# One mixer's slot count, and two weight matrices used unsplit in fp32 products

## The chip, the cores and the metric

The kernel runs on one core of a Trainium2 chip. The metric is device time in microseconds (us) of one execution. The three executions shown of the kernel before took 1184.0, 1187.42 and 1192.24 us; their median is 1187.42 us.

## The reference

Two layers run over 256 tokens of width 1024, all in float32. Each layer is a SwiGLU feed-forward block, a token mixer and a second feed-forward block. Each block has an RMS norm before and after it, and shift, scale and gate vectors computed from a conditioning vector `c` (`silu(c) @ mod_w`). The mixer, in short:

```
proj = h @ w_in                       # cut into u, q, k, v, f, g_a, g_b
y_ssm = s5_ssm(u, ...)                # diagonal state-space scan, 32 groups of 64 states
z_val, z_gate = split(gelu(y_ssm) @ glu_w, 2)
y_a = z_val * sigmoid(z_gate)
attn = forgetting_attention(q, k, v, f + forget_b)      # 8 heads of 64
y_b = attn @ attn_w_out
out = (sigmoid(g_a) * y_a + sigmoid(g_b) * y_b) @ w_out
```

The two matrices that the change touches are `attn_w_out` (512 x 1024) and `glu_w` (512 x 2048), both in layer 0 only.

## The kernel before

**Pieces and their split.** All large weights are cut into pieces of 128 x 1024 float32 (512 KB) and stored in one tensor `ws` in the order in which they are wanted (`stream_order`, line 86). Class `Stream` (line 324) loads them one after the other through SyncE's queue (`pump`, tiles `raw`). A product in nearly full precision is made of three products in the type fp32r: ScalarE copies a piece into its rounded high part (`hi`, line 359), VectorE subtracts it to get the low part (`lo`, line 372), and `out_piece` (line 719) issues high x high, high x low and low x high for each half of 512 columns. The left operand is split in the same way. A piece of `mod_w` (`mod`) is not split: VectorE multiplies it by `silu(c)` and sums (tile `crow`).

**Slots.** Every 4 KB-per-partition tile lives in a pool of 42 slots. `used` counts one slot for a loaded piece and two for a split one. `room` is 42 less `KEPT` (what the current stage keeps for its own tiles) and, while the state-space tables are being built, less `TABLES[stage]`. `pump` loads while `used() < room()` and while fewer than 11 pieces wait loaded; `hi_at` makes no new split once `used() >= room()`, unless at most one split piece is unused.

**Order.** Each engine runs its instructions in the order in which they were written. That order is made while the program is built: class `Plan` keeps an estimated clock for each engine, and generators (`Task`) offer their next step with a rank; `pick` (line 223) takes the one that can start earliest, the lower rank in a tie.

**The mixer of layer 0** (`mix_body`, line 946). After the projections v, ga0, q, k and u, TensorE computes four rounds of attention scores (`sc`). While VectorE and ScalarE do their softmax, it fills in with the gate projections ga1, gb0 and gb1 (tiles `ga`, `gb`, four pieces each; `fill`) and with the state-space inputs `vr`, `vi`. The scan runs on VectorE (`zr`, `zi`); then come the products `ys`, in two halves by `states`, placed between the eight products of the attention output (`yb`, weights `ao`). The gelu of each half moves data in 16 small copies, alternately on VectorE and ScalarE (`gelu`, line 1283), then splits its result (`ygh`, `ygl`). `z` is the GLU product (weights `gl`); it needs gelu's first half for k = 0, 1 and its second from k = 2. Before the last product (`ym`, weights `mo`), `load_rows` (line 492) waits for the mixer's gate vector, and transposes it on TensorE (`gT`).

**The tables.** `s5_tables(0)` (line 1712) runs beside the first feed-forward block and the projections. Near its end `s5_place` writes table `d` to DRAM in 16 small DMAs; `load_tables` reads `bt` and `d` back into six slots; `s5_w` then builds the scan's phases `wc`, `ws` on VectorE, which go through DRAM to the scan.

Of the kernel before, what the change touches and what calls it, by code (L numbers as in the profile page):

```python
# [10 lines left out]
F32R = mybir.dt.float32r  # L11
I32 = mybir.dt.int32
AF = mybir.ActivationFunctionType
ALU = mybir.AluOpType
# [23 lines left out]
KEPT = {"ffn": 10, "mix0": 7, "mix1": 23, "mix2": 22, "mix3": 14, "mix4": 11}  # L38
TABLES = (11, 8)
TICKS = (1, 2)  # L40
# [5 lines left out]
NEAR = 1  # L46
LATER = 4
SCAN, GELU, MERGE, TR = 0.5, 0.95, 0.5, 1.5
# [37 lines left out]
def stream_order():  # L86
    order = []
    first = [("mod", 0, 0, r, k) for k in range(8) for r in (1, 0)]
    order += first[0:2] + [("fi", 0, 0, 0, 0)] + first[2:4]
    for n in range(1, 16):  # L90
        order += [("fi", 0, 0, n % 4, n // 4)] + first[3 + n:4 + n]
    mods = [
        vec(0, 0, 2) + vec(0, 1, 1) + vec(0, 1, 0),
        vec(0, 2, 1) + vec(0, 2, 0) + vec(0, 1, 2),
        vec(1, 0, 1) + vec(1, 0, 0) + vec(0, 2, 2) + vec(1, 1, 1),
        vec(1, 1, 0) + vec(1, 0, 2) + vec(1, 1, 2),
        [],
        vec(1, 2, 2),
    ]
    mods[2] += vec(1, 2, 1) + vec(1, 2, 0)  # L100
    for g in range(6):
        l, s = divmod(g, 3)
        w = sub_weights(l, s, g == 0)
        m = mods[g]
        lo, hi = SPREAD[0 if g == 0 else 1 + s % 2]
        hi += len(w)
        at = [lo + (hi - lo) * i // len(m) for i in range(len(m))]
        n = 0
        for i, key in enumerate(w):
            while n < len(m) and at[n] <= i:  # L110
                order.append(m[n])
                n += 1
            order.append(key)
        assert n == len(m)
    return order


# [206 lines left out]
class Stream:  # L324
    def __init__(self, kb, ws, order):
        self.kb, self.ws, self.order, self.plan = kb, ws, order, kb.plan
        self.dma = 0
        self.kept = KEPT["ffn"]
        self.hurry, self.over = None, []
        self.raw, self.mods, self.split = [], [], []  # L330
        self.live, self.fresh = {}, set()
        ahead = lambda: 0.4 if len(self.fresh) < NEAR else 1 if len(self.fresh) < AHEAD else 4
        Part(self.plan, self.hi_at, self.hi, ahead)
        Part(self.plan, self.lo_at, self.lo, ahead)
        Part(self.plan, self.mod_at, self.mod, self.mod_rank)

    def pump(self, most=None):
        kb, most = self.kb, most or RAW
        while self.dma < len(self.order) and len(self.raw) + len(self.mods) < most and self.used() < self.room():
# [4 lines left out]
            self.plan.floor = None  # L344
            (self.mods if key[0] == "mod" else self.raw).append((key, t))
            self.dma += 1

    def used(self):
        return len(self.raw) + len(self.mods) + 2 * (len(self.live) + len(self.split))

# [48 lines left out]
    def done(self, key):  # L399
        del self.live[key]  # L400
        self.pump()

# [11 lines left out]
class Kern:  # L414
# [304 lines left out]
    def out_piece(self, y, lh, ll, w, first, last):  # L719
        mm = self.nc.tensor.matmul  # L720
        wh, wl = w
        for n in range(2):
# [223 lines left out]
    def mix_body(self):  # L946
# [66 lines left out]
        self.probs_t(sc)  # L1013
        self.at = self.r4("ath", F32R), self.r4("atl", F32R)
        self.values(0, sc)
# [20 lines left out]
        def later_terms():  # L1036

            yg.extend([self.r4("yg"), self.r4("ygh", F32R), self.r4("ygl", F32R)])
            sr, si = s
# [65 lines left out]
        for m in range(2):  # L1105
            yb = self.psum("yb")
            for k in range(4):
                key = ("ao", l, k)
                w = self.st.need(key)
                a = k * 256 + m * P  # L1110
                self.out_piece(yb, self.at[0][:, a:a + P], self.at[1][:, a:a + P], w, k == 0, k == 3)
                if m == 1:
# [12 lines left out]
        for n, ms in ((0, (0, 1)), (1, (0,)), (1, (1,))):  # L1125
            z = {m: self.psum("z") for m in ms}
            for k in range(4):
# [4 lines left out]
                if n == 0 and k % 2 == 0:  # L1132
                    self.finish(late[k // 2])
                    if k == 2:
                        yg.pop(0)
                for m in ms:
                    a = k * 256 + m * P
                    self.out_piece(z[m], yg[-2][:, a:a + P], yg[-1][:, a:a + P], w, k == 0, k == 3)
                if ms[-1] == 1:
# [7 lines left out]
        if not turned:  # L1147
            self.finish(merges[0])
            self.transpose_split(0, [t[:, 0:512] for t in self.sga])
        self.merged = merges[1]  # L1150

    def load_tables(self):
# [130 lines left out]
    def gelu(self, h, ys, out):  # L1283

        nc = self.nc
        w = slice(512 * h, 512 * h + 512)
        y, hi, lo = (t[:, w] for t in out)
        yield "act", ys
# [4 lines left out]
        for b in range(4):  # L1293
            for t in range(4):
# [4 lines left out]
                else:  # L1299
                    yield "dve", g  # L1300
                    nc.vector.tensor_copy(o, i)
        yield "act", y
        nc.scalar.activation(hi, y, AF.Copy)
        yield "dve", hi
        nc.vector.tensor_tensor(lo, y, hi, op=ALU.subtract)

# [55 lines left out]
    def values(self, jt, sc):  # L1362
# [10 lines left out]
        def split():  # L1373
            src = ps.rearrange("p (m t) -> p m t", m=2)[:, :, 384:512]
            oh, ol = (t[:, 256 * jt:256 * jt + 256].rearrange("p (m t) -> p m t", m=2) for t in self.at)
            yield "act", ps
            nc.scalar.activation(oh, src, AF.Copy)
            yield "dve", self.plan.clk["act"] + self.plan.LATENCY
            nc.vector.tensor_tensor(ol, src, oh, op=ALU.subtract)
# [332 lines left out]
    def s5_tables(self, l):  # L1712
# [24 lines left out]
        kt = self.bd = self.cp = self.bc = None  # L1737
        if self.s == 1:
            self.load_tables()
        self.stage = 1  # L1740
# [220 lines left out]
```

## Time and profile before

| | us |
|---|---|
| median of the runs | 1187.42 |
| the profiled execution | 1182.35 |
| its span, first to last instruction | 1180.6 |
| TensorE busy in it | 1140.6 |
| VectorE busy in it | 912.7 |
| ScalarE busy in it | 608.6 |

"Busy" is time in which at least one instruction of the engine was running; in the profile PE is TensorE's products, PEld its weight loads, DVE is VectorE, ACT ScalarE and SP SyncE, whose queue issues the DMAs. Nearly every instruction has line 128, a helper through which all operations pass, so rows are told apart by the names of the tiles. The mean granted clock of TensorE over the span was 0.992 of full speed.

### The profile page before, as it was taken

The numbers are of one execution on the slowest core, as the hardware profiler recorded it, in microseconds if no ns is written. First come the engines' busy times: TensorE is split into PE (matmuls) and PEld (weight loads), VectorE is DVE, ScalarE is ACT, GpSimd is POOL, SyncE is SP. The second block draws the span as 40 slices with busy tenths as digits, with TensorE's granted clock in tenths as the row PEclk, the third lists the DMA queues.
The fourth block names the chain that finished last, engine by engine and source line by source line (L and its number), as shares of the span: only waits on it lengthen the run. The fifth ranks groups of instructions, "written<-read, shape, count | busy, mean of one in ns | idle before, by whom it ended". The sixth has DMA issues, their size and how long they took to land.

```text
span 1180.6 us, 19407 instructions
## 1 busy us (share of the span) xinstructions
PE 1140.6 (97%) x7488; PEld 1015.5 (86%) x7488; DVE 912.7 (77%) x1529; ACT 608.6 (52%) x943; POOL 36.2 (3%) x62
## 2 busy tenths in 40 slices
PE   8999999998998999999999999999999999999997
PEld 5999998796786779999979989987987887999995
DVE  6988987897998889999678878878448798855532
ACT  5653452685556564444364475356355756543421
POOL 1000000000000010000010000001000001000000
PEclk9999999998999999999999999999999999999999
DMA  9999887577887669999769398966645566765300
GB/s 361 408 367 407 301 286 267 187 257 236 339 306 249 224 235 390 360 376 381 246 214 355 127 330 284 373 248 237 227 127 179 180 212 216 284 224 204 126 19 36
DMA packets 99186, 306.50 MB, mean 260 GB/s; under 512 B 16373, under 2 KB 26133, under 8 KB 99094
## 3 DMA queue, kind: packets, MB, share of 16 engines
q1 hardware_dynamic: 99094, 305.27, 71.6%
q8 instruction: 58, 0.95, 0.3%
q14 instruction: 34, 0.28, 0.1%
HBM read 291.51 MB, written 13.71 MB: 259 GB/s over the span
## 4 chain that ended last, share of the span: by engine, by line
PE 86%; DVE 7%; ACT 3%; DMA 2%; issue 2%; POOL 1%; SPq 0%; DVEq 0%; POOLq 0%; ACTq 0%
PE f L128 35%; PE y L128 20%; PE n L128 5%; PE ym L128 3%; PE ga L128 3%; PE gb L128 3%; PE z L128 3%; PE k L128 2%; PE q L128 2%; PE v L128 2%; PE ys L128 2%; PE u L128 2%; ACT xh L128 1%; DVE raw L128 1%; PE yb L128 1%
## 5 line engine op out<-in xcount | busy, mean ns | idle before, releaser
L128 DVE TENSOR_TENSOR lo<-raw,hi 128x1024 fp32r<-128x1024 f32 x368 | 437.1, 1218 | 27.2 <-ACT hi L128 21.3
L128 ACT ACTIVATE hi<-raw 128x1024 fp32r<-128x1024 f32 x367 | 370.7, 1055 | 68.3 <-PE f L128 38.7
L128 PE MATMUL f<-xl,hi 128*128 128x256 f32 x1216 | 341.4, 281 | 2.7 <-DVE xl L128 2.7
L128 PE MATMUL f<-xh,hi 128*128 128x256 f32 x1216 | 342.0, 281 | 1.9 <-ACT xh L128 1.9
L128 PE MATMUL f<-xh,lo 128*128 128x256 f32 x1216 | 341.0, 280 | 0.0
L128 PEld LDWEIGHTS f<-xh,lo 128*128 128x128 f32 x1216 | 232.4, 191 | 0.0
L128 PEld LDWEIGHTS f<-xl,hi 128*128 128x128 f32 x1216 | 228.4, 188 | 4.6 <-DVE xl L128 3.6
L128 PEld LDWEIGHTS f<-xh,hi 128*128 128x128 f32 x1216 | 228.5, 188 | 3.8 <-ACT xh L128 2.5
L128 PE MATMUL y<-hi,ht 128*128 128x512 f32 x704 | 196.2, 391 | 0.8 <-DVE yg L128 0.8
L128 DVE SCALAR_TENSOR_TENSOR raw<-raw,crow 128x1024 f32<-128x1024 f32 x144 | 173.3, 1218 | 6.0 <-DMA raw<-ws 5.9
L128 PEld LDWEIGHTS y<-hi,ht 128*128 128x128 f32 x704 | 129.3, 188 | 26.2 <-DVE yg L128 1.1
L128 ACT ACTIVATE sg<-f 128x512 f32<-128x512 f32 x38 | 22.7, 597 | 222.7 <-PE f L128 215.4
L128 PE MATMUL y<-lo,ht 128*128 128x512 f32 x352 | 109.3, 390 | 0.8 <-ACT yg L128 0.8
L128 DVE TENSOR_TENSOR sg<-sg,f 128x512 f32<-128x512 f32 x38 | 26.1, 687 | 90.0 <-ACT sg L128 89.9
L128 PEld LDWEIGHTS y<-lo,ht 128*128 128x128 f32 x352 | 66.1, 188 | 15.1 <-ACT yg L128 1.2
L128 PE MATMUL n<-hi,xl 128*128 128x512 f32 x96 | 37.9, 395 | 1.7 <-DVE xl L128 1.7
L128 ACT ACTIVATE lg<-lg,st 128x128 f32<-128x128 f32 (+1 forms) x64 | 26.1, 444 | 25.3 <-DVE st L128 25.3
L128 PE MATMUL n<-hi,xh 128*128 128x512 f32 x96 | 38.4, 400 | 0.0
L128 PE MATMUL n<-lo,xh 128*128 128x512 f32 x96 | 37.7, 392 | 0.0
L128 DVE TENSOR_TENSOR yg<-y,row 128x1024 f32<-128x1024 f32 (+1 forms) x9 | 9.9, 1103 | 32.8 <-ACT xn L128 23.6
L128 DVE TENSOR_TENSOR ht<-sg,ht 128x512 fp32r<-128x512 f32 x38 | 26.1, 687 | 9.8 <-ACT ht L128 9.5
L128 ACT ACTIVATE xh<-xt,mc 128x128 fp32r<-128x128 f32 x80 | 21.7, 383 | 22.1 <-PE xt L128 22.1
(276 smaller groups left out, 1646.7 us busy)
## 6 DMA issues: line engine op xcount, KB each, us to landing
raw<-ws SPq DMA_DIRECT2D x512, 512.0 KB, 5.8
row<-sg SPq DMA_DIRECT2D x11, 512.0 KB, 8.0
sbt<-bT SPq DMA_DIRECT2D x8, 512.0 KB, 3.0
sc<-cd SPq DMA_DIRECT2D x16, 256.0 KB, 8.0
bt<-sbt SPq DMA_DIRECT2D x8, 512.0 KB, 4.5
c<-sc SPq DMA_DIRECT2D x8, 512.0 KB, 10.2
d<-sd SPq DMA_DIRECT2D x4, 512.0 KB, 4.6
w<-sw SPq DMA_DIRECT2D x4, 512.0 KB, 5.8
```

The source lines that it names most:

```text
L128: r = f(*a, **k)
```

## The change

In layer 0, `ao` and `gl` pieces go straight from the load to use: `pump` marks them live, they count one slot, and `out_piece` issues one product of plain float32 tiles in place of three fp32r products. The left operands of these products, `at` (attention) and `yg` (gelu), are no longer split in layer 0. `TABLES` goes from (11, 8) to (9, 0). `LATER`, which lowers the mixer's `KEPT` until the tables are loaded, goes from 4 to 15. In the first mixer, `s5_tables` now sets `KEPT` to the mixer's 23 and waits until at most 19 slots are used before it loads the tables.

```diff
-TABLES = (11, 8)
+TABLES = (9, 0)
...
+OVER = 0
-LATER = 4
+LATER = 15
...
+def plain(key):
+    return key[1] == 0 and key[0] in ("ao", "gl")
...
-            (self.mods if key[0] == "mod" else self.raw).append((key, t))
+            if plain(key):
+                self.live[key] = t
+                self.whole += 1
+            else:
+                (self.mods if key[0] == "mod" else self.raw).append((key, t))
...
-        return len(self.raw) + len(self.mods) + 2 * (len(self.live) + len(self.split))
+        return len(self.raw) + len(self.mods) + 2 * (len(self.live) + len(self.split)) - self.whole
...
     def out_piece(self, y, lh, ll, w, first, last):
         mm = self.nc.tensor.matmul
+        if ll is None:
+            for n in range(2):
+                mm(y[:, 512 * n:512 * n + 512], lh, w[:, 512 * n:512 * n + 512], start=first, stop=last)
+            return
...
-        self.at = self.r4("ath", F32R), self.r4("atl", F32R)
+        self.at = [self.r4("at")] if l == 0 else [self.r4("ath", F32R), self.r4("atl", F32R)]
...
+            if not ol:
+                return
+            ol, = ol
             yield "dve", self.plan.clk["act"] + self.plan.LATENCY
             nc.vector.tensor_tensor(ol, src, oh, op=ALU.subtract)
...
         if self.s == 1:
+            self.st.kept = KEPT["mix1"]
+            while self.st.used() > SLOTS - self.st.kept + OVER:
+                yield "dve", self.plan.clk["pe"] + 0.5
             self.load_tables()
```

## Rows read from the trace of the kernel before

**Rows 1.** The page, busy time by engine: busy us (share), instructions

```profile
PE 1140.6 (97%) x7488; PEld 1015.5 (86%) x7488; DVE 912.7 (77%) x1529; ACT 608.6 (52%) x943; POOL 36.2 (3%) x62
```

**Rows 2.** Windows, mixer of layer 0: length, busy PE, PEld, DVE, ACT, POOL; clock; DMA

```profile
262.50:276.90 14.40, 14.40 (x154) 13.07 (x154) 12.02 (x43) 6.69 (x20) 0.00 (x0) 1.00 0.79 266
282.67:291.94 9.27, 5.56 (x13) 4.08 (x14) 9.05 (x49) 6.60 (x16) 1.16 (x2) 0.65 0.45 117
303.30:338.30 35.00, 31.78 (x175) 24.17 (x174) 33.63 (x51) 21.49 (x43) 0.00 (x0) 1.00 0.91 349
366.48:376.00 9.52, 4.73 (x16) 3.81 (x16) 9.43 (x12) 6.57 (x9) 0.00 (x0) 0.82 0.84 264
276.90:393.00 116.10, 99.97 (x554) 81.63 (x553) 104.13 (x213) 70.61 (x130) 1.16 (x2) 0.96 0.81 286
```

**Rows 3.** Waits of TensorE, 276.9 to 394 us: total, times, longest

```profile
PE z L128 <- ACT ygh L128: 4.8, 1, 4.8
PE gT L128 <- DVE mc L128: 2.8, 1, 2.8
PE ga L128 <- DVE lo L128: 2.3, 1, 2.3
PE gb L128 <- DVE lo L128: 1.9, 2, 1.4
PE ga L128 <- ACT hi L128: 1.4, 1, 1.4
```

**Rows 4.** Timeline of weight loads, warming products in fp32: start, length

```profile
14.70 0.19 PEld L128 LDWEIGHTS warm<-warm 128*128 128x128 f32 x1 [0.24 <-issue]
15.13 0.19 PEld L128 LDWEIGHTS warm<-warm 128*128 128x128 f32 x1 [0.24 <-issue]
```

**Rows 5.** Timeline of TensorE, layer 0, ys to z: start, length

```profile
344.04 0.43 PE L128 MATMUL ys<-zr,c 128*128 128x63 f32 x2 [0.64 <-DVE zr L128]
...
352.60 0.70 PE L128 MATMUL yb<-hi,ath 128*128 128x512 f32 x2
...
360.89 0.62 PE L128 MATMUL z<-hi,ygh 128*128 128x512 f32 x2
...
362.25 0.62 PE L128 MATMUL z<-hi,ygh 128*128 128x512 f32 x2
...
371.28 1.22 PE L128 MATMUL z<-hi,ygh 128*128 128x512 f32 x2 [4.79 <-ACT ygh L128]
...
374.00 0.76 PE L128 MATMUL z<-hi,ygh 128*128 128x512 f32 x2
```

**Rows 6.** Timeline of TensorE, third piece of ga1

```profile
286.88 0.79 PE L128 MATMUL ga<-lo,xh 128*128 128x512 f32 x1 [2.28 <-DVE lo L128]
...
291.74 0.63 PE L128 MATMUL sc<-kc,lg 128*128 128x128 f32 x2
```

**Rows 7.** Lines of VectorE, then ScalarE, 276.9 to 393 us: busy, mean ns

```profile
L128 DVE TENSOR_TENSOR lo<-raw,hi 128x1024 fp32r<-128x1024 f32 x28 | 33.5, 1217 | 0.4 <-issue 0.3
...
L128 DVE TENSOR_TENSOR atl<-sc,ath 128x256 fp32r<-128x256 f32 x4 | 1.7, 421 | 3.2 <-ACT ath L128 3.2
...
L128 DVE TENSOR_TENSOR ygl<-yg,ygh 128x512 fp32r<-128x512 f32 x2 | 1.4, 687 | 0.0
...
L128 ACT ACTIVATE yg<-g 32x128 f32<-32x128 f32 x16 | 6.9, 432 | 0.3
```

**Rows 8.** Timeline of SyncE's queue, table writes and loads: start, length

```profile
275.82 12.75 SPq L128 DMA_DIRECT2D sd<-kt  x16
288.62 1.86 SPq L128 DMA_DIRECT2D bt<-sbt  x4
...
291.56 4.34 SPq L128 DMA_DIRECT2D raw<-ws  x5
```

**Rows 9.** Timeline of VectorE, s5_w: last of its first stretch, first after it

```profile
275.81 0.25 DVE L128 TENSOR_TENSOR pw<-pw 128x16 f32<-128x16 f32 x2
...
285.06 0.19 DVE L128 TENSOR_TENSOR wt<-ws,pw 128x32 f32<-128x32 f32 x1
```

More of the change, by code (lines that the diff above doesn't have):

```diff
@@ L330, in __init__ @@
         self.raw, self.mods, self.split = [], [], []
-        self.live, self.fresh = {}, set()
+        self.live, self.fresh, self.whole = {}, set(), 0
         ahead = lambda: 0.4 if len(self.fresh) < NEAR else 1 if len(self.fresh) < AHEAD else 4
@@ L400, in done @@
         del self.live[key]
+        self.whole -= plain(key)
         self.pump()
@@ L1036, in later_terms @@
         def later_terms():
-            yg.extend([self.r4("yg"), self.r4("ygh", F32R), self.r4("ygl", F32R)])
+            yg.append(self.r4("yg"))
+            if l:
+                yg.extend([self.r4("ygh", F32R), self.r4("ygl", F32R)])
             sr, si = s
@@ L1110, in mix_body @@
                 a = k * 256 + m * P
-                self.out_piece(yb, self.at[0][:, a:a + P], self.at[1][:, a:a + P], w, k == 0, k == 3)
+                self.out_piece(yb, *self.halves(self.at, a), w, k == 0, k == 3)
                 if m == 1:
@@ L1133, in mix_body @@
                     self.finish(late[k // 2])
-                    if k == 2:
+                    if k == 2 and l:
                         yg.pop(0)
@@ L1137, in mix_body @@
                     a = k * 256 + m * P
-                    self.out_piece(z[m], yg[-2][:, a:a + P], yg[-1][:, a:a + P], w, k == 0, k == 3)
+                    self.out_piece(z[m], *self.halves(yg[-2:], a), w, k == 0, k == 3)
                 if ms[-1] == 1:
@@ L1150, in mix_body, with halves @@
         self.merged = merges[1]
+    def halves(self, ts, a):
+        out = [t[:, a:a + P] for t in ts]
+        return out if len(out) == 2 else (out[0], None)
     def load_tables(self):
@@ L1286, in gelu @@
         w = slice(512 * h, 512 * h + 512)
-        y, hi, lo = (t[:, w] for t in out)
+        y, *parts = (t[:, w] for t in out)
         yield "act", ys
@@ L1301, in gelu @@
                     nc.vector.tensor_copy(o, i)
[L1302 to L1305, printed above, removed]
+        if parts:
+            hi, lo = parts
+            yield "act", y
+            nc.scalar.activation(hi, y, AF.Copy)
+            yield "dve", hi
+            nc.vector.tensor_tensor(lo, y, hi, op=ALU.subtract)
     def scores(self, jt, qt, kt):
@@ L1374, in split @@
             src = ps.rearrange("p (m t) -> p m t", m=2)[:, :, 384:512]
-            oh, ol = (t[:, 256 * jt:256 * jt + 256].rearrange("p (m t) -> p m t", m=2) for t in self.at)
+            oh, *ol = (t[:, 256 * jt:256 * jt + 256].rearrange("p (m t) -> p m t", m=2) for t in self.at)
             yield "act", ps
             nc.scalar.activation(oh, src, AF.Copy)
+            if not ol:
+                return
+            ol, = ol
             yield "dve", self.plan.clk["act"] + self.plan.LATENCY
```

## The prediction

> **What bounds the kernel now.** First the busy times of the page: TensorE is busy 97% of the span [rows 1], so over the whole program only its own work and its few idle places matter. Next the windows over the mixer of layer 0, which the change edits: between the first ga1 product and the last wait before `ym` (276.9 to 393.0 us), TensorE is busy 99.97 of 116.10 us and VectorE 104.13 [rows 2]. So 16.1 us of TensorE's idle time lie here, and in the middle VectorE is the nearly full engine: 33.63 of 35.00 us between 303.3 and 338.3. Two windows also show the clock granted to TensorE fall after it had stood idle: 0.65 on average in 282.67 to 291.94, 0.82 in 366.48 to 376.00. Of the two levels that is 1.2 GHz for part of each. Then the waits of TensorE [rows 3] name what ended the idle time: the split of the ga1 pieces (1.4 us for a high part, 2.3 for a low part), low parts of gb pieces (1.9), gelu's second half (4.8), the mixer's gate vector (2.8).
>
> **Part 1: fp32 products.** What they cost has to be taken from the warming products at the start, plain fp32 of 128x512. Each is two records, and the loads of consecutive records start at 14.70 and 15.13: 0.43 us, so 0.86 us per product [rows 4]. Three fp32r products of 512 columns take half of the six that lie between 360.89 and 362.25 (two halves): 1.36 / 2 = 0.68 us [rows 5]. Layer 0 has 4 `ao` pieces x 2 row blocks x 2 halves = 16, and 8 `gl` pieces x 2 x 2 = 32, together 48 (a piece times a row block is one piece product of two halves). The cost is 48 x 0.18 = **+8.6 us** on TensorE, all on the path, since TensorE does nothing else in that stretch. Bounds: warming products multiply zeros, and real data may at worst take the full clock away, but nothing here shows that; I keep +8 to +9.
>
> The Trainium skill (FP8 and Floating Point Precision, section TensorE Precision Notes) speaks against this part: true fp32 takes four passes through the array. By it, four passes against three at 0.2267 us each (0.68 / 3) would cost 48 x 0.227 = 10.9 us, an estimate; the row at 0.86 decides, and it already agrees with the rule's direction.
>
> **Part 2: splits that go.** Twelve `hi` and twelve `lo` go, the latter 12 x 1.22 = 14.6 us of VectorE; so do four `atl` (1.7 us) and two `ygl` (1.4 us) with `ygh` [rows 7]. Together 17.7 of VectorE's 104 us in the stretch. None of it is itself on TensorE's path; it counts only through the waits below. The tile `at` is still copied once by ScalarE.
>
> **Part 3: slots during u and ga1.** Before, from the start of u, `KEPT` is 23 - 4 = 19 and `TABLES` 11: room 42 - 19 - 11 = 12, then 42 - 23 - 8 = 11. That is a stock of five pieces, so splits are made just ahead of use. ga1's third piece then waits 1.4 + 2.3 us, and its products run at half speed: eleven between 286.88 and 291.74, 4.86 us [rows 6] for 11 x 0.227 = 2.5. The stall costs 1.4 + 2.3 + 2.4 = **6.1 us**. After the change, room during u is 42 - 8 - 9 = 25, twice as much. VectorE has 2.4 us idle in 262.5 to 276.9 and ScalarE 7.7 [rows 2], and the mod pieces that VectorE does there can be done later. SyncE's queue is closed by table writes from 275.82 to 288.6 [rows 8], so what ga1 and gb0 need until 292 must be loaded before; 13 more slots hold it. I take the whole 6.1 us as gained; bounds 0 to 6.1.
>
> **Part 4: the wait before the table load.** Up to 25 used slots must fall to 19, three pieces consumed: the last of u and two of ga1, until about 276.9 + 2 x 2.9 = 283 us. The reads of `bt` stand behind the 12.75 us of table writes in SyncE's queue and could not start before 288.6 anyway [rows 8], so nothing that reads `bt` or `d` is later. What the wait really delays is `s5_w`, which is created after it. In the trace it has done only a first stretch by 276.1 and goes on at 285.06 [rows 9]: the delay costs what was done in 273.8 to 276.1, 2.3 us, and the ga1 splits that VectorE no longer makes there (two `lo` of 1.22, now made earlier) pay nearly all. Nothing; without that cover +2.3 us on the scan. The scan has room: before, `ys` waits 0.64 us for it and starts at 344.04 [rows 5], with seven of the eight `yb` piece products still to come, which can stand ahead of it.
>
> **Part 5: gb's low parts.** A larger stock and 17.7 us less on VectorE should take half of the 1.9 us: -1.0; bounds 0 to -1.9.
>
> **Part 6: gelu's second half.** This stall costs 4.8 us and, at the lower clock, six products from 371.28 to 374.00 take 2.72 instead of 1.36 [rows 5]: 1.4 more, **6.2 us**. After the change, gelu's second half is asked for later: from `ys`'s end (352.60) TensorE had six `yb` piece products and four of `z` before the wait; each now takes 2 x 0.18 = 0.36 us longer, 3.6 us in all. `ygh`/`ygl` (about 1.3 us) fall out of the chain too. That alone is 4.9 us, more than the wait. Against it: TensorE comes to `ys` about 7 us earlier by parts 3 and 5, uses up `yb` pieces before the scan is done, and then has fewer to put after it. Also the copies of gelu (ScalarE 0.43 us each [rows 7]) were interleaved with splits of `gl`; now pieces of `mo` and mod pieces can take that place. I take -5.0; bounds 0 to -6.2.
>
> **Part 7: the gate vector.** The 2.8 us wait ends when VectorE has done the last mod pieces, which had stood behind splits. With VectorE relieved I take -2.0; bounds 0 to -2.8.
>
> Table counts and `LATER` don't reach layer 1's mixer (its tables are loaded by then); `TABLES` gives its first feed-forward block 2 and 8 more slots, where TensorE is nearly full: nothing, up to 1 us either way from a changed order.
>
> **Sum.** 8.6 - 6.1 - 1.0 - 5.0 - 2.0 = -5.5 us, against the profiled execution of 1182.35: 1176.9. That one lies 5.1 us below the median of the runs; against the median 1187.42 - 5.5 = **1182 us**.
>
> **Rivals.**
> *All stalls go.* -6.1 - 1.9 - 6.2 - 2.8 + 8.6 = -8.4; with the rest of the stretch's 16.1 us idle (16.1 - 4.8 - 2.8 - 3.7 - 1.9 = 2.9) also gone, -11.3: 1176 to 1179. For it: VectorE is relieved by a sixth. Against: those last 2.9 us hang on softmax chains that the change leaves alone. Only with gains elsewhere does it pass 1% (1175.5). Chance 0.25.
>
> *The stock does not grow in time.* At most 11 waiting pieces may be loaded, and VectorE and ScalarE have to split them while they build tables; then ga1 waits as before and the fp32 price shows: 8.6 - 1.0 - 5.0 - 2.0 = +0.6: 1188. The change would not do what its slot count says. Chance 0.15.
>
> *The scan becomes the bound (slower).* TensorE reaches `ys` 7 us earlier than 343.4, at 336.4, and has seven `yb` piece products of 2 x 0.86 = 1.72 us as cover: until 348.4. It decides whether the scan ends after that, 4.4 us later than its 344.04. A late `s5_w` (2.3 us) with four gb splits pulled before it (4.9 us) makes 7.2, so the scan would end at 351. Then TensorE stands idle some 3 us, no `yb` piece product is left to cover gelu, and the two halves of `ys` end at 351 + (352.60 - 344.04) less the one `yb` piece product between them (1.4) = 358. Gelu's second half took 371.28 - 352.60 = 18.7 us; less 1.3 it ends at 375.5, 4.2 us after the old time. The remaining 24 half products add 24 x 0.18 = 4.3, the gate vector gives back 2: +6.5, 1194. Against it: VectorE has fewer splits in that stretch, and the gelu chain need not stay so slow. Chance 0.15.
>
> **How the numbers follow.** The forecast (some of each stall gone, -2 to -8 us) has chance 0.45. One per cent, 11.9 us, is about what a measurement of this kernel can tell from no change. The forecast, the stock rival and most of the scan rival lie within it. Over 1% faster needs the first rival and more: 0.14. Over 1% slower needs the scan rival with a longer stall: 0.06. Same: 0.80. The range takes the first rival less 5 us for runs like the profiled one, and the scan rival's end: 1171 to 1194.
>
> **What would show it.** Products `yb` and `z` of layer 0 with two records of 0.43 us each; no wait of `ga` for `hi` or `lo` and a clock of 1.0 around 282 to 292; `s5_w` starting some 8 us later with `ys` still not waiting long for `zr`; `z`'s wait for gelu (now `yg`) under 2 us; `gT`'s wait shorter; `ym` of layer 0 starting at 386 to 390 instead of 393. The prediction is wrong if `vr`/`vi` wait for `bt`, if `ys` waits for `zr` for more than 3 us, or if fp32 products on real data take more than 0.9 us.

## The result, and the profile after

The changed kernel takes **1196.24 us** (median of 11 runs, 1194.38 to 1197.63) against 1184.0 us of the kernel before on the same chip (11 runs). The ratio is **1.0086, 95% interval 1.0063 to 1.0108**: slower by about 1% (the two medians alone give 1.0103). The forecast was 1182 with a range of 1171 to 1194, so the time lies just above the range and on the other side of no change. The range was reckoned from 1187.42 us, the median of three executions; against the 1184.0 us of all eleven the same -5.5 us would have been 1178.5, so the miss is larger than it looks.

First, where the time went. The windows of both kernels are cut at two products that both have: from the first scores of layer 0's mixer (`sc<-kt`) to the first product with `mo` (`ym`). Columns: length; busy us and count of PE, PEld, DVE, ACT, POOL; granted clock; DMA share; GB/s. The kernel before:

```profile
276.04:393.03 116.99, 100.86 (x563) 82.19 (x562) 104.15 (x214) 71.38 (x131) 1.16 (x2) 0.96 0.81 287
204.00:216.00 12.00, 10.08 (x48) 7.88 (x47) 6.93 (x13) 8.14 (x17) 2.35 (x4) 1.00 0.31 91
```

The busy times of the changed kernel from its page, which answer to those of before [rows 1]:

```profile
PE 1157.0 (97%) x7440; PEld 1014.8 (85%) x7440; DVE 898.5 (75%) x1511; ACT 597.3 (50%) x929; POOL 37.3 (3%) x62
```

And its windows, in the same two stretches:

```profile
277.56:407.20 129.64, 113.95 (x514) 78.30 (x514) 96.49 (x228) 54.27 (x112) 1.25 (x2) 0.89 0.72 261
204.00:216.00 12.00, 10.09 (x40) 7.72 (x40) 7.87 (x14) 6.63 (x15) 2.36 (x4) 0.86 0.52 169
```

The stretch grew from 117.0 to 129.6 us, 12.6 of the 14.9 us between the spans (1180.6 and 1195.5). Of the rest, 1.5 us lie before it (second window; see the end). VectorE has 7.7 us less to do; the forecast counted on 17.7. TensorE's idle time is what it was: 116.99 - 100.86 = 16.1 us before, 129.64 - 113.95 = 15.7 after. Its busy time grew by 13.1: the fp32 price of 8.6 us, and a rest of 4.5 us, which fits a granted clock of 0.89 in place of 0.96: more of the work ran at the lower of the two clock levels.

The waits of TensorE that the change was to take away [rows 3] are gone or small, and another has come. Waits of the changed kernel from 276.9 to 410 us: total, times, longest.

```profile
PE sc L134 <- ACT lg L134: 12.9, 6, 5.8
PE ys L134 <- ACT gb L134: 2.8, 1, 2.8
```

The first of these had a small part before, in the same view as [rows 3]:

```profile
PE sc L128 <- ACT lg L128: 1.1, 2, 1.0
```

`ga` and `gb` wait for no split, `z` no longer waits for gelu and `gT` not for the gate vector: 4.8 + 2.8 + 2.3 + 1.9 + 1.4 = 13.2 us are gone. But the scores now wait 12.9 us for their softmax, in place of 1.1. TensorE's timeline shows where (start, length, in brackets the idle time ahead and what ended it):

```profile
294.30 0.33 PE L134 MATMUL sc<-kc,lg 128*128 128x128 f32 x1 [4.61 <-ACT lg L134]
...
300.34 0.79 PE L134 MATMUL gb<-hi,xh 128*128 128x512 f32 x1
...
329.10 0.93 PE L134 MATMUL sc<-kt,qt 64*128 64x128 f32 x8
...
335.75 0.47 PE L134 MATMUL ys<-U,d 128*128 128x64 f32 x1 [2.77 <-ACT gb L134]
...
352.41 0.48 PE L134 MATMUL sc<-kc,lg 128*128 128x128 f32 x1 [5.81 <-ACT lg L134]
...
363.42 0.33 PE L134 MATMUL ys<-zr,c 128*128 128x63 f32 x2
```

From 300.34 to 314.9 TensorE does five pieces of gb, which before the change stood behind `vr` and `vi`; these now start at 314.71 in place of 295.49, the third round of scores at 329.10 in place of 307.39, and `ys` of the states at 363.42 in place of 344.04 [rows 5]. With gb used up early, nothing is left to fill the fourth round (5.81 us). VectorE's timelines show what stands ahead of the scan. Before, its stretch between `s5_w`'s last step (307.5) and the scan (`zr<-w,vr`):

```profile
308.93 0.34 DVE L128 SCALAR_TENSOR_TENSOR lg<-nbd,cq,sc 128x128 f32<-128x128 f32 x1
...
315.06 1.21 DVE L128 TENSOR_TENSOR zr<-w,vr 128x1024 f32<-128x1024 f32 x1
```

After, from a split (`lo`) that waits for a slot, which the write `sc<-cd` gives free, to the scan:

```profile
276.99 1.23 DVE L134 TENSOR_TENSOR lo<-raw,hi 128x1024 fp32r<-128x1024 f32 x1 [3.90 <-DMA sc<-cd]
...
291.60 0.07 DVE L134 MEMSET wc<- 128x16 f32 x1
...
318.53 1.22 DVE L134 SCALAR_TENSOR_TENSOR raw<-raw,crow 128x1024 f32<-128x1024 f32 x1
...
330.07 0.35 DVE L134 SCALAR_TENSOR_TENSOR lg<-nbd,cq,sc 128x128 f32<-128x128 f32 x1 [2.10 <-PE sc L134]
...
332.75 1.22 DVE L134 SCALAR_TENSOR_TENSOR raw<-raw,crow 128x1024 f32<-128x1024 f32 x1
...
334.92 1.19 DVE L134 TENSOR_TENSOR zr<-w,vr 128x1024 f32<-128x1024 f32 x1
```

The rows `raw<-raw,crow` are pieces of `mod_w`. Seven of them stand between `s5_w`'s end (317.5) and the scan, where before there was none. In this kernel, though, six of the seven are not what the scan waited for: behind them VectorE stands idle for 2.10 us until the third round of scores comes (330.07), and only the seventh stands between that softmax and the scan. Between 240 and 340 us VectorE does twenty pieces in place of ten. Its groups by line show them (busy us, mean ns), first before:

```profile
L128 DVE SCALAR_TENSOR_TENSOR raw<-raw,crow 128x1024 f32<-128x1024 f32 x10 | 11.9, 1217 | 0.2 <-DMA raw<-ws 0.2
```

and after:

```profile
L134 DVE SCALAR_TENSOR_TENSOR raw<-raw,crow 128x1024 f32<-128x1024 f32 x20 | 24.6, 1260 | 0.0
```

SyncE's timeline shows the larger room as loads (`raw<-ws`) that stand ahead of small transfers [rows 8] (start, time to issue):

```profile
278.96 0.33 SPq L134 DMA_DIRECT2D nbp<-snb  x1
...
281.58 6.60 SPq L134 DMA_DIRECT2D raw<-ws  x7
288.49 13.91 SPq L134 DMA_DIRECT2D sd<-kt  x16
302.49 1.80 SPq L134 DMA_DIRECT2D bt<-sbt  x4
305.47 12.74 SPq L134 DMA_DIRECT2D raw<-ws  x10
...
320.45 0.33 SPq L134 DMA_DIRECT2D sw<-ws  x1
...
329.32 1.55 SPq L134 DMA_DIRECT2D w<-sw  x2
```

The same way of the phases through DRAM before the change:

```profile
307.51 0.33 SPq L128 DMA_DIRECT2D sw<-ws  x1
309.62 1.62 SPq L128 DMA_DIRECT2D w<-sw  x2
```

The softmax's mask (`nbp`) is read 6.5 us later than before (272.41), the table writes `sd` start 12.7 us later and the read of `bt` 13.9. The phases `w` are read 8.9 us after their write in place of 2.1, and the second of them lands at 335.79 (before: 316.73), when the scan's second product, at 336.03, needs it. So two things that are late end together at the scan: the third softmax, behind TensorE's changed order, and `w`, behind the loads.

### The profile page after: what moved, and what is told of

It is laid out like the page before. It is cut to its first block, busy times and chain, and to the rows that moved or that the text cites. A ratio compares the mean times of both kernels' runs of the same rounds, so it can differ in the third digit from the quotient of the medians.

```text
span 1195.5 us, 19271 instructions
## 1 busy us (share of the span) xinstructions
PE 1157.0 (97%) x7440; PEld 1014.8 (85%) x7440; DVE 898.5 (75%) x1511; ACT 597.3 (50%) x929; POOL 37.3 (3%) x62
## 4 chain that ended last, share of the span: by engine, by line
PE 87%; DVE 5%; ACT 3%; DMA 2%; issue 1%; POOL 1%; SPq 0%; DVEq 0%; POOLq 0%; ACTq 0%
PE f L134 35%; PE y L134 18%; PE n L134 4%; PE gb L134 4%; PE z L134 4%; PE ym L134 3%; PE ga L134 3%; PE yb L134 2%; PE ys L134 2%; PE v L134 2%; PE k L134 2%; PE q L134 2%; PE sc L134 2%; ACT xh L134 1%; DVE lo L134 1%
## 5 line engine op out<-in xcount | busy, mean ns | idle before, releaser
L134 DVE TENSOR_TENSOR lo<-raw,hi 128x1024 fp32r<-128x1024 f32 x356 | 424.1, 1219 | 36.6 <-ACT hi L134 21.6
L134 ACT ACTIVATE hi<-raw 128x1024 fp32r<-128x1024 f32 x355 | 359.6, 1056 | 91.3 <-PE f L134 47.6
```

The lines of the kernel that those rows point to most:

```text
L134: r = f(*a, **k)
```

## The experiments

Ratios are against the kernel before on the same chip, with their 95% interval. Several readings competed: **Q**, that SyncE's queue alone makes the tables late; that the planner's **order** ahead of `vr` and `vi` (five gb pieces) does; that the low **clock** does; that a **larger room** does by whatever fills it; and at last that the pieces of `mod_w` on VectorE (**mod pieces**) do.

**The two halves of the change.** The first run keeps the fp32 products and takes back the slot edits; the second does the reverse.

```diff
# e1_fp32_only: against the changed kernel
-TABLES = (9, 0)
+TABLES = (11, 8)
-LATER = 15
+LATER = 4
-            self.st.kept = KEPT["mix1"]
-            while self.st.used() > SLOTS - self.st.kept + OVER:
-                yield "dve", self.plan.clk["pe"] + 0.5
# e2_slots_only
-    return key[1] == 0 and key[0] in ("ao", "gl")
+    return False
...
```

> Only the first part of the change: layer 0's ao and gl pieces unsplit in fp32 products; TABLES (11, 8), LATER 4 and no wait before the table load, as in the kernel before. Theory Q (the weight loads that the larger room lets into SyncE's queue delay the tables, and with them the scan): the table writes start near 276 us and the products ys near 344 as before, z no longer waits for gelu, and the time is 1184 - 2 to 1184 + 4 us: 8.5 us of fp32 products against some 8 us of stalls. Rival P (the fp32 products themselves are the loss): 8 to 12 us slower than before, as the whole change.

> Only the other part: TABLES (9, 0), LATER 15 and the wait before the table load; all weights and left operands are split as before. Theory Q: the table writes start near 288 us, the scan ends 15 us or more later than before, and the kernel is 4 to 12 us slower than before although ga1 no longer waits. Rival P: 1 to 6 us faster than before, since the ga1 stall of 6 us goes and nothing is added.

Measured: fp32 only 0.9999 (0.9977 to 1.0021), slots only 1.0039 (1.0020 to 1.0058). The window from first scores to `ym` of fp32 only:

```profile
276.45:393.25 116.80, 107.55 (x515) 73.12 (x514) 92.19 (x201) 57.54 (x115) 1.17 (x2) 0.97 0.79 297
```

Its waits of TensorE from 276 to 410 us:

```profile
PE gb L134 <- DVE lo L134: 4.4, 2, 3.9
PE ga L134 <- DVE lo L134: 2.3, 1, 2.3
PE sc L134 <- ACT lg L134: 1.0, 1, 1.0
```

The window of slots only:

```profile
275.71:397.69 121.98, 105.35 (x563) 85.24 (x562) 106.79 (x241) 65.54 (x125) 1.90 (x2) 0.90 0.74 268
```

Its waits of TensorE in that stretch:

```profile
PE sc L134 <- ACT lg L134: 11.7, 7, 4.5
PE z L134 <- ACT ygh L134: 2.4, 1, 2.4
PE z L134 <- DVE ygl L134: 0.8, 1, 0.8
```

With fp32 only, TensorE's busy time grows by 6.7 us and its idle time falls by 6.9 (16.1 to 9.3): `z` and `gT` wait no more, and the scores wait 1.0 us for their softmax, as before. With slots only they wait 11.7 us, and TensorE's busy time grows by 4.5 us without a single new product. The half that was to bring the gain is the half that loses, and it has the same late order as the whole change (five gb pieces ahead of `vr`, third scores at 327.80). The two do not add: fp32 costs nothing on the kernel before and about 1.0086 - 1.0039 = 0.5% on top of the slots. There the stall that it takes away (`z` for gelu, 3.2 us) is smaller than its price.

**One slot edit at a time.** `LATER` back to 4 in the whole change; `LATER` 15 as the only slot edit, on top of fp32 only; the second number of `TABLES` as the only one (the room after the tables are loaded, 8 slots more); the last both with all fp32 products and with those of `gl` only.

```diff
# e3_later4: whole change          # e9_later15_alone: e1 and
-LATER = 15                        -LATER = 4
+LATER = 4                         +LATER = 15
# e10_room_after_tables: e1 and    # e11_glu_only: e1 and
-TABLES = (11, 8)                  -    return key[1] == 0 and key[0] in ("ao", "gl")
+TABLES = (11, 0)                  +    return key[1] == 0 and key[0] == "gl"
# e12_glu_only_room: e11 and
-TABLES = (11, 8)
+TABLES = (11, 0)
```

> The whole change but LATER 4 in place of 15, so that fewer weight loads stand ahead of the table writes in SyncE's queue (four behind the mask loads in place of eight, and one less ahead of them). Theory Q: the table writes start 4 to 7 us earlier than in the changed kernel, the scan follows, and the time falls by 3 to 8 us from the changed kernel's 1196. Rival P: within 2 us of the changed kernel.

> The fp32 products with the old TABLES (11, 8) and no wait, and LATER 15: only the room during the u projection grows. Theory S (the larger room before the tables are loaded is the harm: more splits and mod pieces run on VectorE ahead of the first softmax round, more loads stand ahead of the tables, and the plan spends five gb pieces ahead of vr/vi): ga has no wait, softmax round 0 waits 4 us or more, TensorE's clock is at its lower level for 15 us or more in the mixer, and the kernel is 8 to 13 us slower than before. Rival T (the TABLES numbers do it): within 3 us of the kernel before.

> The fp32 products with LATER 4, no wait, and TABLES (11, 0): the room grows only once the tables are loaded. Theory S: the order of TensorE is that of the fp32 products alone, gb's wait for low parts (4.4 us there) shrinks to about 1 us, and the kernel is 1 to 5 us faster than before the change. Rival T: 5 us or more slower, as the changed kernel.

> Only the gl pieces are unsplit in fp32 products; ao is split as before; TABLES (11, 8), LATER 4, no wait. Gelu's stall lies at z, so the 16 fp32 products of ao buy nothing but VectorE time: without them TensorE has 2.9 us less to do, and if nothing waits for the four ao splits the kernel is 2 to 4 us faster than with both (1183.5) and than before. If the four splits and atl come into the way again: no gain.

> gl alone in fp32 products, and TABLES (11, 0). Theory S: both gains together, 3 to 7 us faster than before the change. Rival T: 5 us or more slower.

Measured: `LATER` back 1.0077 (1.0049 to 1.0104); `LATER` alone 1.0138 (1.0098 to 1.0177); room after the tables 1.0050 (1.0027 to 1.0073); `gl` only 0.9969 (0.9940 to 0.9997); `gl` only with that room 1.0044 (1.0019 to 1.0069). The two runs with more room after the tables were expected to be faster: both missed. `LATER` back was to give 3 to 8 us by the queue reading, and gave nothing that the intervals show. Eight more slots after the table load cost 0.5% with all fp32 products and 0.75% with `gl` alone, and the waits of `LATER` alone show the same place, 19.5 us of it:

```profile
PE sc L134 <- ACT lg L134: 19.5, 6, 10.4
```

So both edits that were run alone, `LATER` and the second number of `TABLES`, are a loss by themselves; the first number and the wait before the table load were not run alone. In the runs with room after the tables the loss has another place: ten or eleven weight loads go out ahead of the phases, `w` is read 7.3 and 8.9 us after its write (e12, e10) in place of 2.2 (fp32 only), and in e12 the scan waits 0.98 us for `w`. That is the queue reading, by way of the phases. Unsplitting `gl` alone is the better part of the change; with `ao` unsplit too the ratio is 0.9999 in place of 0.9969, for another 2.9 us of products, though the intervals of the two overlap.

**The queue and the order.** In layer 0 the 16 writes of `sd` go to GpSimd's queue (e4); or the fill with gate pieces ahead of `vr` and `vi` is left out (e5); or both (e6); or both, with the mask's three transfers on GpSimd's queue as well (e7); or both without fp32 (e8).

```diff
# e4, and in e6 to e8
-                self.nc.sync.dma_start(d[32 * s:32 * s + 32, :, j, 32 * s:], ...
+                q = self.nc.sync if l else Timed(self.plan, "dma", self.nc.raw.gpsimd)
+                q.dma_start(d[32 * s:32 * s + 32, :, j, 32 * s:], ...
# e5, and in e6 to e8
-        self.fill(lambda: self.begun() and self.there(*bt[0], *bt[1])())
+        if l:
+            self.fill(lambda: self.begun() and self.there(*bt[0], *bt[1])())
```

> The whole change, with the 16 writes of table d issued on GpSimd's queue in place of SyncE's; every engine's other instructions keep their order. This frees 13 us of SyncE's queue. If the late bt is what holds the scan: bt is read near 289 instead of 302 and the time falls by 5 to 10 us. If the phases' way through DRAM behind the weight loads holds it (what I expect under theory Q): the scan starts at most 4 us earlier and the time falls by 0 to 4 us. Rival P: no change.

> The whole change, but in layer 0 TensorE goes from the second round of scores straight to vr and vi: the call of fill that puts gate pieces there until the plan holds bt for loaded is left out. Theory O (the changed kernel loses because the plan, which sees the tables late, spends five gb pieces ahead of vr/vi, so the later softmax rounds and the scan start 20 us later and find nothing to fill with): the third round of scores starts near 312 us in place of 329, ys near 350 in place of 363, and the time falls by 5 to 10 us from the changed kernel, though vr must wait some 5 us for bt, which is still read near 302. Theory Q (the queue alone): vr waits and nothing is gained, within 2 us of the changed kernel's 1196.

> As the kernel before it (no gate pieces ahead of vr/vi), and the 16 writes of table d on GpSimd's queue, so that bt is read near 288 us. Theory O: no wait for bt is left, ys starts near 345 and the kernel is 2 to 6 us faster than before the change: the ga1 stall and gelu's stall are gone against 8.5 us of fp32 products. Theory Q: 2 to 5 us faster than with the fill left out alone. Rival P (fp32 is the loss): still 5 us or more slower than before.

> As the kernel before it, with the three small mask transfers (store, two broadcasts) on GpSimd's queue too, so that they don't stand behind weight loads in SyncE's queue. If the first softmax round waits for the mask (its products wait 5.9 us for it in the changed kernel): another 2 to 4 us faster. If it is the softmax chain itself: no difference.

> The slot part of the change alone (all splits kept), with no gate pieces ahead of vr/vi and the writes of table d on GpSimd's queue. Theory O: the ga1 stall is gone, gelu's stall stays and nothing is added: 3 to 7 us faster than before the change. If fp32's relief of VectorE is what pays: slower than the same with fp32 products.

Measured: e4 1.0092 (1.0064 to 1.0120), e5 1.0172 (1.0142 to 1.0202), e6 1.0115 (1.0086 to 1.0143), e7 1.0099 (1.0071 to 1.0127), e8 1.0011 (0.9987 to 1.0036). e5 to e8 were each expected to be faster by 2 us or more, by the order reading, and none is; e5 is slower than the changed kernel. In e4 `bt` is read at 288.08 in place of 302.49, `vr` still starts only at 313.23 behind five gb pieces, and nothing is gained: the late tables are not enough as a cause. In e6 `vr` starts at 297.79, 17 us earlier than in the changed kernel, and the scan still only at 327.05; five or six mod pieces stand between `s5_w` and the scan in each of e5 to e8. The place of gb ahead of `vr` is not enough as a cause either. e8's interval touches that of slots only, so no gain is shown there.

e7 shows the pieces in the way of the scan. Its third scores come at 309.07, nearly as early as before the change (307.39), and `w` is read 2.9 us after its write. From the chain of work that ended last (start, length):

```profile
313.42 1.14 DVE lo L134
314.55 5.72 DVE raw L134 x10
320.28 1.55 DVE lg L134 x6
```

Five mod pieces, 5.7 us (each is two records there), stand ahead of the softmax of scores that are long done, without idle time, and the scan starts at 326.21. In the same view of the changed kernel the softmax follows on the scores themselves, which came last:

```profile
329.17 0.88 PE sc L134 x8
330.07 1.64 DVE lg L134 x6
```

So where the scores come early the pieces hold the softmax, and where they come late the scores do. Taking away one late thing left the other.

**The clock.** TensorE's waits are filled with products of 128x512 whose result is overwritten: in the whole change 18 ahead of the first softmax round's transposes and 20 ahead of the fourth's (e13); in e10, 8 ahead of `vr` (e14); in e6, 18 and 8 (e16).

```diff
+    def heat(self, out, n):
+        for _ in range(n):
+            self.nc.raw.tensor.matmul(out, self.xh[:, 0, 0, :], ..., start=True, stop=True)
...
+            self.heat(ps[:, 0:512], (18, 0, 0, 20)[self.round])     # e13; e16: (18, 0, 0, 0)
+            self.heat(vr[:, 0:512], 8)                              # e14, e16
```

> The whole change, with products whose result is thrown away put where TensorE waits for softmax rounds 0 and 3 of layer 0: 18 and 20 products of 512 columns (4.1 and 4.6 us at full clock). Nothing else moves. Theory C (the idle time of the changed kernel is as long as before, 16 us, but lies so that TensorE's clock stays at its lower level for 28 us of the mixer in place of 9): with the waits filled, the lower level falls below 18 us and the kernel gets 3 to 8 us faster than the changed one, by work that does nothing. Rival D (the late scan is all): no gain, or a loss by the products that overrun the waits.

> The fp32 products with TABLES (11, 0) (1191.5 us), and eight products that are thrown away, into vr's tile, just ahead of vr/vi, where TensorE waits 0.9 us for bt and then runs vr/vi at half clock. Theory C: vr/vi take 7 to 9 us in place of 12, and the kernel is 3 to 8 us faster than without them. Rival D (w, loaded 7 us later behind weight loads, holds the scan): no gain.

> The whole change with no gate pieces ahead of vr/vi and the writes of table d on GpSimd's queue (1199.7 us, 34 us of the mixer at half clock), and products that are thrown away: 18 where softmax round 0 is waited for, 8 ahead of vr/vi. In the changed kernel filling the waits gained nothing, since the late scan came last there. With the gate pieces taken away from vr/vi, TensorE itself comes last, so theory O and the clock together expect vr/vi in 7 to 9 us in place of 14, less than 20 us at half clock, and 1186 to 1192 us. If the scan still comes last: within 2 us of 1199.7.

Measured: e13 1.0097 (1.0078 to 1.0115), e14 1.0048 (1.0032 to 1.0063), e16 1.0102 (1.0063 to 1.0142). The window from first scores to `ym` of e13:

```profile
276.18:404.19 128.01, 120.03 (x553) 83.08 (x552) 96.66 (x228) 54.07 (x112) 1.25 (x2) 0.95 0.72 264
```

The same of e10:

```profile
276.22:403.18 126.96, 115.70 (x514) 80.45 (x514) 92.02 (x200) 56.23 (x114) 1.16 (x2) 0.89 0.73 274
```

And of e14:

```profile
275.44:398.62 123.18, 110.89 (x522) 75.80 (x522) 92.06 (x201) 56.24 (x114) 1.17 (x2) 0.94 0.76 281
```

Between levels of 1 and 1/2, a mean clock c means a share 2(1 - c) at the lower level: 28.5 us of the changed kernel's stretch, about 13 of e13's, and yet its time is no better. In e14 the profiled stretch is 3.8 us shorter than in e10, but the ratios are level (1.0050 and 1.0048). e16, expected at 1186 to 1192 us, took 1200.0 (median). A faster TensorE did not help where what it waits for comes late. In e14 the scan waits 0.52 us for `w`, which was read 8.9 us after its write: the run's other theory, that `w` behind weight loads holds the scan, fits.

**Half of `gl`.** Only the four pieces of `gl` for `z`'s first half stay unsplit, without the slot edits.

```diff
# e15_glu_half: e11 and
-    return key[1] == 0 and key[0] == "gl"
+    return key[1] == 0 and key[0] == "gl" and key[2] == 0
```

> As the kernel with gl alone in fp32 (1180 us), but only the first four of the eight gl pieces, those whose products stand at gelu's stall; the other four and their left operand are split as before. TensorE has another 2.9 us less to do. If the stall goes with the first four alone: 1 to 4 us faster than gl alone, 4 to 7 us faster than before the change. If the four splits come into gelu's way again: no gain over gl alone.

Measured: **1178.98 us, 0.9963 (0.9946 to 0.9980)**, faster than both kernels. Its window from first scores to `ym`:

```profile
276.39:386.77 110.38, 101.47 (x547) 77.61 (x546) 100.58 (x213) 65.67 (x126) 1.18 (x2) 0.98 0.85 308
```

Of its waits of TensorE in that stretch none is of `z`; that of `gT`:

```profile
PE gT L134 <- DVE mc L134: 0.2, 1, 0.2
```

It pays for 16 fp32 products (2.9 us) and still gets back `z`'s stall and all but 0.2 us of `gT`'s. From `gl` alone (0.9969) it can't be told apart.

**The mod pieces.** The last two runs leave the numbers of the room as they are and hold VectorE back from pieces of `mod_w`, unless nine wait, from u until the scan is on its queue: in the whole change (e17), and in e15 with the slot edits added (e18).

```diff
     def mod_at(self):
+        if self.hold and len(self.mods) < 9:
+            return None, 0.0
...
+        self.st.hold = l == 0
         pu = self.psum("u")
...
         self.finish(value)
+        self.st.hold = False
         sc = self.scores(2, qt, kt)
```

> The whole change, but from u on VectorE takes a piece of mod_w in layer 0 only when nine of them wait, until the scan has been put on its queue. In the order that VectorE is given, 50 mod pieces stand ahead of the scan in place of 64 (56 before the change), one between s5_w's end and the scan in place of seven, and one gb piece ahead of vr and vi in place of five. Theory of the mod pieces (the larger room is filled with mod pieces, VectorE multiplies them where the scan's work stood, and the plan then pushes gb pieces ahead of vr and vi): the scan starts at 312 to 320 us in place of 334.9, first scores to ym takes 115 to 121 us in place of 129.6, and the ratio is 0.995 to 1.003. Theory that a larger room is a loss by its queue of loads or by low clock whatever VectorE does: the scan starts after 324 and the ratio stays 1.006 to 1.010. Third theory, that the pieces only come back later: the scan starts by 320 but gT waits for mc by more than 3 us, ratio 1.002 to 1.006.

> Only the first four gl pieces unsplit, the slot edits of the change as they are, and mod pieces held back as in the run before. Theory of the mod pieces: 0.991 to 0.997, level with the same kernel without the slot edits (0.9963) or better. Theory that a larger room is a loss whatever VectorE does: 1.002 to 1.008, as the slot edits alone gave 1.0039.

Measured: e17 1184.72 us, **0.9992 (0.9967 to 1.0016)**; e18 1198.65 us, 1.0108 (1.0073 to 1.0143). VectorE's line of mod pieces from 240 to 340 us in e17:

```profile
L134 DVE SCALAR_TENSOR_TENSOR raw<-raw,crow 128x1024 f32<-128x1024 f32 x6 | 7.2, 1221 | 0.0
```

Its window from first scores to `ym`:

```profile
277.44:397.60 120.16, 112.25 (x515) 76.60 (x514) 99.04 (x234) 53.29 (x111) 1.37 (x2) 0.93 0.77 282
```

And its timeline of VectorE, the last mod piece and the start of the scan:

```profile
315.78 1.22 DVE L134 SCALAR_TENSOR_TENSOR raw<-raw,crow 128x1024 f32<-128x1024 f32 x1
...
320.74 1.21 DVE L134 TENSOR_TENSOR zr<-w,vr 128x1024 f32<-128x1024 f32 x1
```

With the slots, the wait and the fp32 products all in place, the loss of the change is gone: 1.0086 becomes 0.9992, and the intervals lie apart. The stretch takes 120.2 us in place of 129.6, and the scan starts 14.2 us earlier (just outside the 312 to 320 that was expected). Holding the pieces back is enough to undo the loss here.

The run does not show by which way, since a held piece also keeps its slot: up to eight slots are taken by pieces that wait, and fewer loads go out. Three go out between the read of `d` and the phases in place of ten, and `w` is read 2.1 us after its write in place of 8.9. The plan also puts one gb piece ahead of `vr` in place of five, and four loads ahead of `sd` in place of eight (281.33 in place of 288.49). These last two can be ruled out as enough: `LATER` back (e3) also has one gb piece ahead of `vr`, four loads ahead of `sd` (281.57) and its third softmax at 318.55 (e17: 318.06), and it still loses 0.8%. Its scan starts at 328.85, 8.1 us after that of e17. What it has and e17 has not is five mod pieces in place of one between `s5_w` and the scan, and eleven loads ahead of the phases, with `w` read 8.9 us after its write. Which of the two costs more no run separates: none holds the pieces while it lets the loads go, or the other way round.

e18 missed. Its waits from 270 us on:

```profile
PE gT L134 <- DVE mc L134: 8.5, 1, 8.5
PE yb L134 <- DVE lo L134: 4.9, 1, 4.9
```

The scan starts early there too (319.43), but the pieces held back come due later, beside splits of `ao` and half of `gl` that e17 does not have: seven of them stand from 395.72 to 403.8, right ahead of `mc`, for which `gT` waits until 404.37. That is the third theory of e17's expectation. So the hold is no cure by itself; it moves work, and here the work came back in another place.

## Why the prediction was wrong, step by step

- **Part 1, the fp32 products: right.** The chain of work that ended last has 32 records of `z` in 13.73 us, 0.86 us per product of two records, as taken from the warming products [rows 4]; real data cost no more. From slots only to the whole change TensorE's busy time grows from 105.35 to 113.95, the 8.6 us of the sum (from before to fp32 only, 6.7). The Trainium skill (FP8 and Floating Point Precision, section TensorE Precision Notes) has four passes for true fp32; the 10.9 us estimated from that in the prediction are more than the 8.6 measured, and only its direction agrees.

```profile
379.31 13.73 PE z L134 x32
```

- **Part 2: right as a count, wrong in one clause of part 3 that leans on it.** VectorE has 7.7 us less in the stretch, not 17.7. Of the ten that are missing 3.2 are mod pieces (9.5 us became 12.7), some 2.5 are two splits that moved in (28 became 18, not 16), and 2.3 are `s5_w`'s first steps, which had stood before it.
- **Part 3, the slots during u and ga1: the step that failed.** The stalls of ga1 did go, so the room came in time. But the sum books the larger room as a gain of 6.1 us and puts nothing against it; the rivals say that the softmax chains are left alone by the change, and part 3 that VectorE's mod pieces "can be done later". Neither held. TensorE's wait for its softmax rounds grew from 1.1 to 12.9 us, with slots only 11.7 and with fp32 only 1.0, and the slot half, forecast at -6.1, measured 1.0039, some 4.6 us slower. That much is shown by taking the two halves apart. What the room did on the way: it was filled in load order, mod pieces among the rest, and the plan, which takes what can start earliest, let VectorE do them as they landed, ten more by 340 us (11.9 us became 24.6). More loads stood ahead of the small transfers, the mask and the phases. And a split waited 3.90 us for a slot ahead of the first softmax round, where TensorE then stood idle 4.61 us, 5.9 with the round's other waits. e17 shows that keeping mod pieces back undoes the loss; how much of it is VectorE's time and how much the loads that then stay out is open. That part of the cause is argued and not shown.
- **Part 4, the wait before the table load: wrong.** "Nothing that reads `bt` or `d` is later" overlooked that the 16 writes of `d` themselves stand in SyncE's queue behind whatever `pump` has put there: eight loads after the change, two before. `bt` was read 13.9 us later. `s5_w`, which the wait was to delay by 2.3 us of work, starting some 8 us later, started at 291.60 in place of 273.8, 18 us later, and ended 10 us later. e4 shows that the late `bt` alone did not set the time, and `vr` did not wait for `bt` in the changed kernel: TensorE was given gb pieces in its place.
- **Part 5: right.** gb waits for no split (1.9 us gained; -1.0 taken).
- **Part 6: right in mechanism.** `z` has no wait for gelu, with the slots or without; e1, e11 and e15 give the stall back whole. In the changed kernel it stands behind a scan that ends at 362.3 in place of 344.0.
- **Part 7: right.** `gT` does not wait in the mixer of layer 0, in place of 2.8 us.

The sum without part 3 is 8.6 - 1.0 - 5.0 - 2.0 = +0.6 us, the figure of the stock rival, and fp32 only measured 0.9999: the parts on the products and their stalls add up, the part on the slots does not. The rival "the scan becomes the bound" came nearest: it put the scan's end at 351 and the time at 1194, against 362.3 and 1196. Its mark (scan later than 348.4) was passed, but its way there was another: `s5_w` ended 10 us later, the scan began 20 us later, behind the late third softmax and the late `w`, and TensorE had no wait for the scan. That its 1194 came near is luck. It was given 0.15, because the argument against it counted the splits that VectorE loses and not the pieces that more room brings. The other two marks named did not show: neither `vr` nor `ys` of the states waited long, because the planner had moved other work in front of them. A late producer showed as a changed order instead of as a wait. The forecast also took 1% for what a measurement here can just tell from no change; the intervals reach 0.2 to 0.4% to either side.

## What to carry to other kernels

More buffers did not only take waits away here: whatever came next in the load order filled them, those loads stood ahead of small transfers that the stage needed, and the work that hangs on them ran early, in front of the stage's own chain. Before giving a stage more room, list what will be loaded into it, which transfers will stand behind it and on which engine the work lands. Holding back what was not due turned 1.0086 into 0.9992 here, but not in e18, where the held work came due ahead of a wait. And when several things are late from one source, a run that mends one of them can show nothing (e4, e7, e13), which does not clear it. A product that costs more on TensorE can still pay if it frees an engine that TensorE waits for, but only as far as there is a wait to give back: half of `gl` gained 0.4%, all of `gl` and `ao` gained nothing that the interval shows.

## What the runs showed of the hardware

- **The clock after the same stall was not the same in every execution.** At 206 to 209 us TensorE waits 0.5 and 1.5 us for its input, in both kernels alike. In the window 204 to 216 the granted clock was then 1.00 in the kernel before and 0.86 in the changed one, whose v products ran at 1.2 GHz from 209.2 on (48 records in the window against 40, 8 x 0.227 = 1.8 us of work). Of the eighteen experiments, the profiles of five show 0.86 there (e3, e12, e15, e16, e17) and those of thirteen 1.00. This is about the 1.5 us that the stretch before the mixer lost. No edit explains it: e13 is the changed kernel up to its first thrown-away products, behind 277 us, has 1.00 there, and its first scores come at 276.18 as against 277.56.
- **So too after the wait for `bt`.** In e10 TensorE waits 0.93 us for `bt` behind the first pair of these 64-column products, and `vr` and `vi` take 13.22 us with a mean granted clock of 0.62, from 296.5 us at the lower level to their end. In e12 it waits 0.86 us at the same place, and they take 8.41 us at 1.00. In fp32 only, without that wait, they take 7.44 us at 1.00. The window of e10:

```profile
293.58:306.80 13.22, 12.29 (x67) 12.18 (x66) 11.58 (x47) 3.35 (x12) 0.52 (x2) 0.62 1.01 393
```

- **Small transfers stood behind prefetched weights.** The 16 strided writes of `sd` took 12.75 us to issue before and 13.91 after. The mask's store (`snb`) was issued 3.95 us later than before (272.23 as against 268.28), behind a weight load of 2.35 us and with its rows ready 1.4 us later, and its read (`nbp`) followed 6.7 us after the store in place of 4.1. The phases needed 8.9 us from write to read in place of 2.1, after ten loads of 512 KB each.
